# A hybrid decoder trunk on one core: one-pass split products for the index scores, and another order for queries, taps, norm and sparse heads

## The chip, the cores and the metric

The kernel runs on one core of one Trainium2 chip. The metric is the device time of one execution in microseconds (us); the time before is the median of three runs.

## The reference

Two layers over 256 tokens of width 2048, float32. Each layer normalises `x`, multiplies it with one wide input matrix and splits the product into the inputs of three branches and their gates. What the change touches is branch A's token index, the sparse attention behind it, and the place of branch B's norm and branch C's heads around them.

```python
proj = h @ w_in
(qa, ka, va, za, qi, ki, wi, ub, zb, qc, kc, vc, zc, gates) = split(proj)
qa, ka, qi, ki = rope(qa), rope(ka), rope(qi), rope(ki)        # 8, 2, 16 and 1 heads of 128
# A: blocks of 128 queries, each sees the keys up to the block's end
rel   = einsum('bthd,bsd->bhts', qi, ki)                       # 16 index heads, one index key
score = einsum('bhts,bth->bts', relu(rel), wi)
score = where(causal, score, -1e30)
idx   = top_k(score, 64)                                       # each query keeps 64 keys
y_a   = softmax attention of qa over the kept ka, va           # 8 heads, 2 key heads
# B: GLU, causal depthwise conv of 31 taps, LayerNorm, swish
# C: stick-breaking attention, 8 heads
x = x + (g0*(y_a*silu(za)) @ w_a + g1*(y_b*silu(zb)) @ w_b + g2*(y_c*silu(zc)) @ w_c) @ w_out
```

A query among the first 64 has at most 64 causal keys, so it keeps all of them, whatever their scores.

## The kernel before, in words

**Products.** Nearly all matmuls are split products: each operand is written as a high and a low part in a one-pass float32 type (F32R), and a product is high x high + low x high + high x low, three one-pass matmuls that accumulate in PSUM. Weights stream in units of up to 512 KB: a DMA on SP's queue fills a raw buffer (six of them), ScalarE (ACT) casts it to the high part (`high`, L264), VectorE (DVE) subtracts to get the low part (`low`, L269), and TensorE (PE) multiplies (`mult`, L280). High and low parts have three buffers each. `chunk_W`, `chunk_N` give 512 or fewer columns token by token, `chunk_T` gives heads transposed (`rope` rotates these). Small products, those of the index among them (L820), are plain float32 matmuls on unsplit operands.

**Order.** The program order is written out by hand, and a scheduler then orders each engine's instructions by priority. Casts and subtractions run at high priority. Work off the projections goes into three lists. `turns` and `stages` hold generators: after each unit `background` lets one of them go a step (turns first, then the first two stages), bound behind that unit's last matmul; `yield n` asks for n more units. `waiting` holds the 31 taps of the convolution for each half of the channels (`taps`: four ACT scalings L442 and one DVE add L445 each); after a unit's subtraction `drain` issues one of them, unless `hold` is set. `settle`, `finish` and `flush` issue what is left of each list. `turn_in` transposes a chunk with DMAs on SP's queue (L178) between a step before and one after.

**A layer's sequence, as far as the change goes.** Gate and value chunks of branch B and queries, keys, values of branch C (taps begin to drain); four stick generators (two heads each) are started; `hold` is set; index key (2 units), values of A with the index weights (8 units), keys of A (4 units), queries of A (two `chunk_W` of 16 units in all, each turned in and rotated by `spin`, L796 to L798); `finish`; the 16 index query heads as eight `chunk_T` of four units, for the 192 tokens from 64 on, each rotated at once by `rope`; `hold` is lifted; two index generators are started, one for each block of queries; two gate chunks (`early`, 16 units); `finish`; four attention generators (`attend`); two more gate chunks; `flush` of the taps; the conv norm generator; the gates `ZC` and `ZB` (32 units). The index generators take four heads at a step:

```python
for q in range(4):
    nc.tensor.matmul(ps[:, q * n:(q + 1) * n], at(qiT, hd)[:, t * P:(t + 1) * P],
                     kiT[:, 0, :n], start=True, stop=True)      # n = 128 or 256 keys
```

and add each head's relu, times its weight, to the scores; then eight rounds of eight maxima pick the 64 keys. SBUF comes from pools: twelve slots `s8`, eight `t4` temporaries, three `ev`.

Of the kernel before, what the change touches and what calls it, by code (L numbers as in the profile page):

```python
# [15 lines left out]
P = 128  # L16
S = 256
# [37 lines left out]
def trunk(ctx: ExitStack, tc: tile.TileContext, x, xt, w_in, w_a, w_b, w_c, w_out,  # L55
# [33 lines left out]
    sin2 = heads(cst[:, C_SIN:C_SIN + S], 2)  # L89

    uid = [0]

# [73 lines left out]
    def turn_in(src, dst, then=None, slots=True, turn=TURN, early=False):  # L166
        own, cols = words(slots)
        rows = own.rearrange("p (t w d) -> p t w d", t=NT, w=2)
        s16 = src.bitcast(U16).rearrange("p t (d w) -> p t d w", w=2)
        with tc.high_priority():  # L170
            for i in range(2):
                nc.scalar.copy(rows[:, :, i, :], s16[:, :, :, i])

        def steps():
            yield turn[0]
            with tc.high_priority() if turn in MERGED else nullcontext():
                for t in range(NT):
                    nc.sync.dma_start(cols.rearrange("p (g t) -> p g t", g=8)[:, :, t * P:(t + 1) * P],  # L178
                                      own[:, t * 1024:(t + 1) * 1024], transpose=True)
            yield turn[1]  # L180
            halves_ = cols.rearrange("p (w f t) -> p w f t", w=2, f=4)
            into = own.bitcast(F32).rearrange("p (f t) -> p f t", f=4) if dst is None else dst
            d16 = into.bitcast(U16).rearrange("p f (t w) -> p f t w", w=2)
            bound = turn == LATE or turn in MERGED
            with tc.issue_after(lows[0].ins) if bound else nullcontext(), tc.high_priority() if bound else nullcontext():
                nc.vector.tensor_copy(d16[:, :, :, 1], halves_[:, 1])
            with tc.issue_after(highs[0].ins) if bound else nullcontext(), tc.high_priority() if bound else nullcontext():
                (nc.vector.tensor_copy if early else nc.scalar.copy)(d16[:, :, :, 0], halves_[:, 0])
            if dst is None:
                then(into, cols.bitcast(F32).rearrange("p (f t) -> p f t", f=4))  # L190
            elif then is not None:
                then()

        turns.append([steps(), count[0] + 0])
        advance(turns[-1])
# [4 lines left out]
    def finish():  # L200
        while stages:
            advance(stages[0])
# [189 lines left out]
    def split(h, l, src):  # L392
        nc.scalar.copy(h, src)
        nc.vector.tensor_sub(l, src, h.bitcast(F32))
# [1 line left out]
    def pair(n):  # L396
        return tuple(tp.tile([P, n], F32R, tag=t, bufs=2, name=nm(t)) for t in ("ph", "pl"))

    def rope(acc, dst):
        a, a3 = summed(acc)  # L400
        nh, nt = a3.shape[1:]
        sw = ev()[:, :nh * nt]
        with tc.high_priority():
            nc.scalar.copy(sw[0:64, :], a[64:128, :])
# [4 lines left out]
            nc.vector.tensor_add(dst, dst, s3)  # L409

    def sigmoid_of(a):
        sg = ev()
        with tc.high_priority():
            nc.scalar.activation(sg, a, AF.Sigmoid)
        return sg.rearrange("p (h t) -> p h t", h=2)

    def gate(c0, o, b, w, hx, park=None, slots=True, turn=TURN):
        def gated(k, z, v):
# [71 lines left out]
    for layer in range(DEPTH):  # L490
# [288 lines left out]
        va_ = t4(F32R).rearrange("p (i t d) -> p i t d", i=2, t=NT)  # L779
        va = [va_[:, i] for i in range(2)]  # L780
        wi = small(NT * NIH, 2).rearrange("p (t h) -> p t h", t=NT)
        a = chunk_N(w, [(O_VA, 256), (O_WI, NIH)], hx, KD)
        for t in range(NT):
            with tc.high_priority():
                split(va[0][:, t, :], va[1][:, t, :], a[t][:, :256])
                nc.scalar.mul(wi[:, t, :], a[t][:, 256:256 + NIH], WI_SCALE)
        rope(chunk_T(w, O_KA, 256, hx, KD), kaT)

        qaT = slot()
        def spin(q4):  # L790
            for h in range(0, 4, 2):
# [19 lines left out]
        def index(t, qiT=qiT, kiT=kiT, wi=wi, bias=bias):  # L811
            n = (t + 1) * P
            cb = cst[:, C_CB + S - n:C_CB + S]
            sc = tp.tile([P, S], F32, tag="sc", bufs=2, name=nm("sc"))
            bs = tp.tile([P, S], F32, tag="bias", bufs=2, name=nm("bias"))
            for g in range(NIH // 4):
                ps = mm_tile()
                for q in range(4):
                    hd = g * 4 + q
                    nc.tensor.matmul(ps[:, q * n:(q + 1) * n], at(qiT, hd)[:, t * P:(t + 1) * P],  # L820
                                     kiT[:, 0, :n], start=True, stop=True)
                rl = t4()
                nc.scalar.activation(rl[:, :4 * n], ps[:, :4 * n], AF.Relu)
                for q in range(4):
                    hd = g * 4 + q
                    nc.vector.scalar_tensor_tensor(sc[:, :n], rl[:, q * n:(q + 1) * n], wi[:, t, hd:hd + 1],
                                                   cb if hd == 0 else sc[:, :n], op0=ALU.mult, op1=ALU.add)
                yield 2
            for _ in range(TOPK // 8):
                m8 = small(8)  # L830
                nc.vector.max(m8, sc[:, :n])
                nc.vector.match_replace(sc[:, :n], m8, sc[:, :n], TAKEN)
            nc.vector.tensor_scalar(bs[:, :n], sc[:, :n], -2e38, NEG, op0=ALU.is_gt, op1=ALU.mult)
            nc.vector.tensor_tensor(bs[:, :n], bs[:, :n], cb, op=ALU.min)
            bias[t] = bs

        for t in range(NT):
            start(index(t))

        def early(b, j):  # L840
            a = chunk_N(w, [(O_G + b * D + j * 512, 512)], hx, KD)
# [57 lines left out]
        for t in range(NT):  # L899
            for c in range(2):  # L900
                start(attend(t, c))


        for j in range(2, 4):
            early(1, j)
        flush()
        def conv_norm(cv=cv, pr=pr):
            work = t4()
# [22 lines left out]
            for i in range(2):  # L931
# [7 lines left out]
                    nc.vector.tensor_scalar(cs[:, c, :], cs[:, c, :], lw, lb, op0=ALU.mult, op1=ALU.add)  # L939
                nc.vector.tensor_mul(cs, cs, sg.rearrange("p (c t) -> p c t", c=4))  # L940
        start(conv_norm())
        gate(O_ZC, qcT, [], w, hx, parked[2])
        gb = []
        gate(O_ZB, cv, gb, w, hx, slots=False, turn=LATE)
# [308 lines left out]
```

## Time and profile before

| what | value |
|---|---|
| median of 3 runs | 2019.54 us (2019.14 to 2019.95) |
| profiled execution: span from first to last instruction | 2016.9 us |
| PE busy | 2005.8 us (99%) |
| PE weight load busy | 1699.3 us (84%) |
| DVE busy | 1577.9 us (78%) |
| ACT busy | 1388.3 us (69%) |
| POOL busy | 104.8 us (5%) |
| mean granted TensorE clock | 0.999 |

The span runs from the first to the last instruction of the profiled execution; for that execution no other time is given, and the median of the runs is 2.6 us above it. Engines run beside each other, so the shares do not add up. A busy PE is not a PE at its best pace, since matmuls overlap: their pace is read from start to start. A chain row has a start, a duration and what ran; a window row has the stretch, its length, then for each engine busy us and the number of instructions, the clock, the DMA share and GB/s. A group row ends with busy us and the mean ns of one, and the idle time before it.

### The profile page before, as it was taken

How to read it: one execution, taken by the hardware profiler on the slowest of the kernel's cores; microseconds unless marked ns; L12 is line 12 of the kernel's file. 1: busy time of each engine (PE TensorE's matmuls, PEld its weight loads, DVE VectorE, ACT ScalarE, POOL GpSimd, SP SyncE). 2: the span in 40 equal slices, each digit the busy share in tenths (PEclk: the TensorE clock that was granted, in tenths of full speed). 3: DMA queues.
4: the chain of work that ended last, by engine and by line, in shares of the span. 5: the costliest groups of instructions: out<-in, count | busy, mean ns of one | idle time of the engine just before them, and what ended most of it. 6: DMA issues, size and time to landing. Idle time of an engine off the chain costs nothing.

```text
span 2016.9 us, 26722 instructions
## 1 busy us (share of the span) xinstructions
PE 2005.8 (99%) x9550; PEld 1699.3 (84%) x9550; DVE 1577.9 (78%) x1750; ACT 1388.3 (69%) x1952; POOL 104.8 (5%) x160
## 2 busy tenths in 40 slices
PE   9999999999999999999999999999999999999998
PEld 7888889988888888888888888899888888888887
DVE  8688767897798888866676887678967988788665
ACT  7899666687776555556658986676877765555653
POOL 0000000000001200110000000000000012002100
PEclk9999999999999999999999999999999999999999
DMA  8787666656988877889867775676678789768983
GB/s 285 215 227 213 179 178 204 214 178 195 253 237 261 272 245 236 262 267 263 267 198 216 217 211 175 177 205 209 188 206 255 227 261 302 219 230 273 283 268 126
DMA packets 340278, 458.66 MB, mean 227 GB/s; under 512 B 109104, under 2 KB 159024, under 8 KB 340016
## 3 DMA queue, kind: packets, MB, share of 16 engines
q1 hardware_dynamic: 327040, 420.88, 69.7%
q0 software_dynamic: 11648, 33.56, 5.1%
q10 hardware_dynamic: 1456, 2.51, 0.4%
q8 instruction: 75, 1.23, 0.2%
q14 instruction: 59, 0.48, 0.1%
HBM read 413.37 MB, written 20.97 MB: 215 GB/s over the span
## 4 chain that ended last, share of the span: by engine, by line
PE 98%; DMA 1%; DVE 0%; ACT 0%; issue 0%; ACTq 0%; SPq 0%; DVEq 0%
PE acc L280 87%; PE mm L280 8%; PE mm L820 1%; PE mm L857 1%; PE mm L895 0%; PE mm L764 0%; PE mm L728 0%; DMA s<-s 0%; DMA raw<-in_w_in_dram 0%; DVE wl L269 0%; PE mm L750 0%; PE mm L731 0%; PE mm L766 0%; PE mm L755 0%; PE mm L752 0%
## 5 line engine op out<-in xcount | busy, mean ns | idle before, releaser
L280 PE MATMUL acc<-wh,s 128*128 128x512 f32 (+2 forms) x4736 | 1157.0, 386 | 1.2 <-ACT wh L264 1.1
L269 DVE TENSOR_TENSOR wl<-raw,wh 128x1024 fp32r<-128x1024 f32 (+2 forms) x714 | 857.2, 1207 | 294.8 <-ACT wh L264 277.0
L280 PEld LDWEIGHTS acc<-wh,s 128*128 128x128 f32 x4736 | 875.6, 188 | 177.4 <-ACT wh L264 1.5
L264 ACT CAST wh<-raw 128x1024 fp32r<-128x1024 f32 (+2 forms) x713 | 738.8, 1039 | 387.3 <-PE acc L280 304.5
L280 PE MATMUL acc<-wl,s 128*128 128x512 f32 (+2 forms) x2368 | 622.6, 385 | 0.0
L280 PEld LDWEIGHTS acc<-wl,s 128*128 128x128 f32 x2368 | 439.5, 188 | 89.1 <-DVE wl L269 0.2
L442 ACT ACTIVATE t<-s,cst 128x255 f32<-128x255 f32 (+14 forms) x480 | 199.9, 487 | 0.0
L445 DVE TENSOR_TENSOR s<-s,t 128x1020 f32<-128x1020 f32 (+14 forms) x120 | 138.4, 1153 | 0.0
L280 PE MATMUL acc<-s,wh 128*128 128x384 f32 (+1 forms) x608 | 125.8, 348 | 0.0
L280 PE MATMUL mm<-wh,s 128*128 128x512 f32 x448 | 119.7, 389 | 0.0
L280 PEld LDWEIGHTS acc<-s,wh 128*128 128x128 f32 x608 | 104.2, 189 | 3.2
L280 PEld LDWEIGHTS mm<-wh,s 128*128 128x128 f32 x448 | 84.1, 188 | 17.4
L231 POOL COPY sm<-sm 128x3 f32<-128x3 f32 x64 | 52.6, 821 | 544.6 <-ACT sm L230 544.6
L280 PEld LDWEIGHTS acc<-s,wl 128*128 128x128 f32 x608 | 79.0, 191 | 1.9 <-DVE wl L269 0.9
L280 PE MATMUL acc<-s,wl 128*128 128x192 f32 (+1 forms) x608 | 79.5, 273 | 0.6 <-DVE wl L269 0.6
L264 ACT CAST wh<-s 128x1024 fp32r<-128x1024 f32 x32 | 33.6, 1049 | 66.1 <-DVE s L1046 58.6
L280 PE MATMUL mm<-wl,s 128*128 128x512 f32 x224 | 69.1, 390 | 0.0
L264 ACT CAST wh<-t 128x1024 fp32r<-128x1024 f32 x32 | 33.6, 1050 | 40.5 <-DVE t L1046 28.0
L269 DVE TENSOR_TENSOR wl<-s,wh 128x1024 fp32r<-128x1024 f32 x32 | 39.2, 1225 | 24.0 <-ACT wh L264 23.7
L280 PEld LDWEIGHTS mm<-wl,s 128*128 128x128 f32 x224 | 41.9, 188 | 9.0 <-DVE wl L269 0.4
L269 DVE TENSOR_TENSOR wl<-t,wh 128x1024 fp32r<-128x1024 f32 x32 | 39.1, 1222 | 9.9 <-ACT wh L264 7.1
L1046 DVE TENSOR_TENSOR t<-raw,raw 128x1024 f32<-128x1024 f32 x32 | 39.0, 1219 | 0.0
(220 smaller groups left out, 1260.6 us busy)
## 6 DMA issues: line engine op xcount, KB each, us to landing
raw<-in_w_in_dram SPq DMA_DIRECT2D x570, 512.0 KB, 4.4
raw<-in_w_out_dram SPq DMA_DIRECT2D x64, 512.0 KB, 5.1
raw<-in_w_b_dram SPq DMA_DIRECT2D x32, 512.0 KB, 5.1
raw<-in_w_c_dram SPq DMA_DIRECT2D x32, 512.0 KB, 5.2
raw<-in_w_a_dram SPq DMA_DIRECT2D x32, 512.0 KB, 5.3
parked<-s POOLq DMA_DIRECT2D x16, 512.0 KB, 4.7
t<-gates POOLq DMA_DIRECT2D x16, 512.0 KB, 7.0
s<-parked POOLq DMA_DIRECT2D x32, 256.0 KB, 5.7
```

What stands on the lines that cost most here:

```text
L231: seen = nc.gpsimd.tensor_copy(copy[:, :3], mark)
L264: highs[0] = nc.scalar.copy(u[1], u[0])
L269: sub = nc.vector.tensor_sub(u[2], u[0], u[1].bitcast(F32))
L280: newest[0] = nc.tensor.matmul(o, lhsT, rhs, start=start, stop=stop, skip_group_check=True)
L442: nc.scalar.activation(o[:, i, :S - d], yT[:, c, :S - d], AF.Copy, scale=wq)
L445: nc.vector.tensor_add(to, to, o[:, :, :S - d])
L820: nc.tensor.matmul(ps[:, q * n:(q + 1) * n], at(qiT, hd)[:, t * P:(t + 1) * P], kiT[:, 0, :n], start=True, stop=True)
L857: nc.tensor.matmul(ps[:, q * n:(q + 1) * n], qaT[:, c * 4 + q, ts_], kaT[:, c, :n], start=True, stop=True)
L1046: nc.vector.tensor_tensor(o, a_, b_, op=op)
```

## The change

It does four things.

1. The index scores become split products in the one-pass type. Index key and index queries are split into high and low parts; each product is three matmuls. The block of the first 128 queries computes only queries 64 to 127 and puts two heads side by side into one stationary tile (`index_near`); its scores come out on two halves of the partitions and are added. The other block keeps its shape (`index_far`).
2. The rotation of the index queries moves out of `rope` into a generator `rotate`, four heads at a time, whose steps run in `turns`, one after each unit; it ends with the split.
3. The two query chunks of the sparse attention go ahead of the index key, values and keys; `hold` is set only behind all of them, so that taps are drained beside the stick generators.
4. The conv norm generator starts ahead of the attention generators, and the taps are flushed before them.

```diff
-        hold[0] = True
-        kk_ = t4()
-        kaT = kk_[:, :2 * S].rearrange("p (c t) -> p c t", c=2)
-        kiT = kk_[:, 2 * S:3 * S].rearrange("p (c t) -> p c t", c=1)
-        rope(chunk_T(w, O_KI, P, hx, KD), kiT)
...
         for h in range(0, NH, 4):
             turn_in(chunk_W(w, O_QA + h * P, hx), qaT[:, h:h + 4, :], partial(spin, qaT[:, h:h + 4, :]))
+        kaT = t4()[:, :2 * S].rearrange("p (c t) -> p c t", c=2)
+        ki = tp.tile([P, 2 * S], F32R, tag="ki", bufs=1, name=nm("ki")).rearrange("p (i c t) -> p i c t", i=2, c=1)
+        rope(chunk_T(w, O_KI, P, hx, KD), None, partial(split, ki[:, 0], ki[:, 1]))
...
+        wp_ = small(NIH // 2 + 1, 2)[:, :NIH // 2]
+        wf = wi[:, 0, :].rearrange("p (g q) -> p g q", q=2)
+        nc.scalar.copy(wp_[0:64], wf[64:128, :, 0])
+        nc.scalar.copy(wp_[64:128], wf[64:128, :, 1])
+        rope(chunk_T(w, O_KA, 256, hx, KD), kaT)
+
+        hold[0] = True
         finish()
-        qiT = big()
-        for b in qiT:
-            nc.gpsimd.memset(b[:, :, :TOPK], 0.0)
+        qa2 = slot(F32R).rearrange("p a b -> p (a b)").rearrange("p (i h t) -> p i h t", i=2, h=NIH)
+        qb2 = [slot(F32R).rearrange("p a b -> p (a b)").rearrange("p (h t) -> p h t", h=NIH) for _ in range(2)]
+
+        nq = S - TOPK
+
+        def rotate(h, v4):
+            w4 = t4()[:, :4 * nq].rearrange("p (h t) -> p h t", h=4)
+            yield 1
+            nc.scalar.copy(w4[0:64], v4[64:128])
+            nc.scalar.copy(w4[64:128], v4[0:64])
+            nc.vector.tensor_mul(v4, v4, cos4[:, :, TOPK:])
+            yield 1
+            nc.vector.tensor_mul(w4, w4, sin4[:, :, TOPK:])
+            nc.vector.tensor_add(v4, v4, w4)
+            yield 1
+            hs = slice(h, h + 4)
+            nc.scalar.copy(qa2[:, 0, hs, :], v4[:, :, :TOPK])
+            nc.scalar.copy(qb2[0][:, hs, :], v4[:, :, TOPK:])
+            yield 1
+            nc.vector.tensor_sub(qa2[:, 1, hs, :], v4[:, :, :TOPK], qa2[:, 0, hs, :].bitcast(F32))
+            nc.vector.tensor_sub(qb2[1][:, hs, :], v4[:, :, TOPK:], qb2[0][:, hs, :].bitcast(F32))
+
         for h in range(0, NIH, 2):
-            rope(chunk_T(w, O_QI + h * P, 256, hx, KD, TOPK), qiT[h // KC][:, h % KC:h % KC + 2, TOPK:])
+            if h % 4 == 0:
+                v4 = t4()[:, :4 * nq].rearrange("p (h t) -> p h t", h=4)
+            total(chunk_T(w, O_QI + h * P, 256, hx, KD, TOPK), v4[:, h % 4:h % 4 + 2, :])
+            if h % 4:
+                turns.append([rotate(h - 2, v4), count[0]])
+                advance(turns[-1])
+        settle()
         hold[0] = False
...
+        three = ((0, 0), (0, 1), (1, 0))
+
+        def index_near(qa2=qa2, ki=ki, wp_=wp_, bias=bias):
...
+            for g in range(2):
+                ps = mm_tile()
+                for q in range(4):
+                    h = g * 8 + q * 2
+                    for n, (i, j) in enumerate(three):
+                        nc.tensor.matmul(ps[:, q * P:(q + 1) * P], qa2[:, i, h:h + 2, :], ki[:, j, 0, :P],
+                                         start=n == 0, stop=n == 2)
+                rl = t4()
+                nc.scalar.activation(rl[:, :4 * P], ps[:, :4 * P], AF.Relu)
+                for q in range(4):
+                    nc.vector.scalar_tensor_tensor(sc[:, :P], rl[:, q * P:(q + 1) * P],
+                                                   wp_[:, g * 4 + q:g * 4 + q + 1], sc[:, :P],
+                                                   op0=ALU.mult, op1=ALU.add)
+                yield 2
...
+        def index_far(qb2=qb2, ki=ki, wi=wi, bias=bias):
...
             for g in range(NIH // 4):
                 ps = mm_tile()
                 for q in range(4):
-                    hd = g * 4 + q
-                    nc.tensor.matmul(ps[:, q * n:(q + 1) * n], at(qiT, hd)[:, t * P:(t + 1) * P],
-                                     kiT[:, 0, :n], start=True, stop=True)
+                    for n, (i, j) in enumerate(three):
+                        nc.tensor.matmul(ps[:, q * S:(q + 1) * S], qb2[i][:, g * 4 + q, :], ki[:, j, 0, :],
+                                         start=n == 0, stop=n == 2)
...
+        start(index_near())
+        start(index_far())
...
-        for t in range(NT):
-            for c in range(2):
-                start(attend(t, c))
-
-
-        for j in range(2, 4):
-            early(1, j)
         flush()
...
         start(conv_norm())
+        for t in range(NT):
+            for c in range(2):
+                start(attend(t, c))
+
+
+        for j in range(2, 4):
+            early(1, j)
         gate(O_ZC, qcT, [], w, hx, parked[2])
```

More of the change, by code (lines that the diff above doesn't have):

```diff
@@ L89, in trunk @@
     sin2 = heads(cst[:, C_SIN:C_SIN + S], 2)
+    cos4 = heads(cst[:, C_COS:C_COS + S], 4)
+    sin4 = heads(cst[:, C_SIN:C_SIN + S], 4)
     uid = [0]
@@ L397, in pair, with rope @@
         return tuple(tp.tile([P, n], F32R, tag=t, bufs=2, name=nm(t)) for t in ("ph", "pl"))
-    def rope(acc, dst):
+    def rope(acc, dst, halves=None):
         a, a3 = summed(acc)
         nh, nt = a3.shape[1:]
+        dst = a3 if dst is None else dst
         sw = ev()[:, :nh * nt]
@@ L409, in rope @@
             nc.vector.tensor_add(dst, dst, s3)
[L411 to L415, printed above, removed]
+            if halves is not None:
+                halves(dst)
     def gate(c0, o, b, w, hx, park=None, slots=True, turn=TURN):
@@ L772, in trunk @@
             start(stick(h0))
-        hold[0] = True
-        kk_ = t4()
-        kaT = kk_[:, :2 * S].rearrange("p (c t) -> p c t", c=2)
-        kiT = kk_[:, 2 * S:3 * S].rearrange("p (c t) -> p c t", c=1)
-        rope(chunk_T(w, O_KI, P, hx, KD), kiT)
[L779 to L782, printed above, removed]
-        for t in range(NT):
[L784 to L787, printed above, removed]
         qaT = slot()
@@ new lines, in trunk @@
+        rope(chunk_T(w, O_KI, P, hx, KD), None, partial(split, ki[:, 0], ki[:, 1]))
+        va_ = t4(F32R).rearrange("p (i t d) -> p i t d", i=2, t=NT)
+        va = [va_[:, i] for i in range(2)]
+        wi = small(NT * NIH, 2).rearrange("p (t h) -> p t h", t=NT)
+        a = chunk_N(w, [(O_VA, 256), (O_WI, NIH)], hx, KD)
+        for t in range(NT):
+            with tc.high_priority():
+                split(va[0][:, t, :], va[1][:, t, :], a[t][:, :256])
+                nc.scalar.mul(wi[:, t, :], a[t][:, 256:256 + NIH], WI_SCALE)
@@ L808, in trunk, with chosen @@
+        for h in range(0, NIH, 2):
+            if h % 4 == 0:
[5 more added lines that the diff above has]
+        settle()
         hold[0] = False
         bias = {}
-        def index(t, qiT=qiT, kiT=kiT, wi=wi, bias=bias):
-            n = (t + 1) * P
-            cb = cst[:, C_CB + S - n:C_CB + S]
+        def chosen(sc, bs, cb):
+            for _ in range(TOPK // 8):
+                m8 = small(8)[-sc.shape[0]:]
+                nc.vector.max(m8, sc)
+                nc.vector.match_replace(sc, m8, sc, TAKEN)
+            nc.vector.tensor_scalar(bs, sc, -2e38, NEG, op0=ALU.is_gt, op1=ALU.mult)
+            nc.vector.tensor_tensor(bs, bs, cb, op=ALU.min)
@@ new lines, in trunk @@
+        three = ((0, 0), (0, 1), (1, 0))
+        def index_near(qa2=qa2, ki=ki, wp_=wp_, bias=bias):
+            cb = cst[:, C_CB + P:C_CB + S]
+            sc = tp.tile([P, S], F32, tag="sc", bufs=2, name=nm("sc"))
+            bs = tp.tile([P, S], F32, tag="bias", bufs=2, name=nm("bias"))
+            nc.vector.tensor_copy(sc[:, :P], cb)
+            nc.vector.memset(sc[:TOPK, :P], 0.0)
+            for g in range(2):
[12 more added lines that the diff above has]
+                yield 2
+            near, even = sc[TOPK:, :P], sc[TOPK:, P:]
+            nc.scalar.copy(even, sc[:TOPK, :P])
+            nc.vector.tensor_add(near, near, even)
+            nc.vector.tensor_copy(bs[:TOPK, :P], cb[:TOPK])
+            chosen(near, bs[TOPK:, :P], cb[TOPK:])
+            bias[0] = bs
@@ L814, in index @@
+        def index_far(qb2=qb2, ki=ki, wi=wi, bias=bias):
+            cb = cst[:, C_CB:C_CB + S]
             sc = tp.tile([P, S], F32, tag="sc", bufs=2, name=nm("sc"))
@@ L818, in index @@
                 for q in range(4):
-                    hd = g * 4 + q
-                    nc.tensor.matmul(ps[:, q * n:(q + 1) * n], at(qiT, hd)[:, t * P:(t + 1) * P],
-                                     kiT[:, 0, :n], start=True, stop=True)
+                    for n, (i, j) in enumerate(three):
+                        nc.tensor.matmul(ps[:, q * S:(q + 1) * S], qb2[i][:, g * 4 + q, :], ki[:, j, 0, :],
+                                         start=n == 0, stop=n == 2)
                 rl = t4()
-                nc.scalar.activation(rl[:, :4 * n], ps[:, :4 * n], AF.Relu)
+                nc.scalar.activation(rl, ps, AF.Relu)
                 for q in range(4):
                     hd = g * 4 + q
-                    nc.vector.scalar_tensor_tensor(sc[:, :n], rl[:, q * n:(q + 1) * n], wi[:, t, hd:hd + 1],
-                                                   cb if hd == 0 else sc[:, :n], op0=ALU.mult, op1=ALU.add)
+                    nc.vector.scalar_tensor_tensor(sc, rl[:, q * S:(q + 1) * S], wi[:, 1, hd:hd + 1],
+                                                   cb if hd == 0 else sc, op0=ALU.mult, op1=ALU.add)
                 yield 2
[L829 to L838, printed above, removed]
+            chosen(sc, bs, cb)
+            bias[1] = bs
+        start(index_near())
+        start(index_far())
         def early(b, j):
@@ L897, in attend @@
             nc.scalar.copy(qaT[:, c * 4:c * 4 + 4, ts_], po[:, :512].rearrange("p (h t) -> p h t", h=4))
-        for t in range(NT):
-            for c in range(2):
-                start(attend(t, c))
-        for j in range(2, 4):
-            early(1, j)
         flush()
@@ L941, in trunk @@
         start(conv_norm())
+        for t in range(NT):
+            for c in range(2):
+                start(attend(t, c))
+        for j in range(2, 4):
+            early(1, j)
         gate(O_ZC, qcT, [], w, hx, parked[2])
```

## The prediction

> **What bounds the kernel now.** I read the page first: span, busy shares, shares of the chain that ended last.
>
> ```profile
> span 2016.9 us, 26722 instructions
> PE 2005.8 (99%) x9550; PEld 1699.3 (84%) x9550; DVE 1577.9 (78%) x1750; ACT 1388.3 (69%) x1952; POOL 104.8 (5%) x160
> PE 98%; DMA 1%; DVE 0%; ACT 0%; issue 0%; ACTq 0%; SPq 0%; DVEq 0%
> ```
>
> PE carries 98% of the chain. Then the waits, PE's own (all there are) and two of ACT's:
>
> ```profile
> PE acc L280 <- ACT wh L264: 1.1, 1, 1.1
> PE mm L625 <- DVE eps L76: 1.1, 1, 1.1
> PE acc L280 <- DVE wl L269: 0.6, 1, 0.6
> ...
> ACT wh L264 <- PE acc L280: 314.1, 254, 3.4
> ACT wh L264 <- DMA raw<-in_w_in_dram: 8.1, 6, 1.7
> ```
>
> PE waits 2.8 us in all, 2.2 of it at the start. The casts of ACT wait for PE to give a weight buffer back (314.1 us), hardly for a load (8.1 us). So a matmul taken out of PE's stream is worth its pace, and work on ACT, DVE, POOL or SP is worth nothing until it makes PE wait. The execution is the profiled one, 2016.9 us of span; the median of the runs is 2019.54, so 2.6 us lie around the span. I apply differences to the median.
>
> **The sum on PE.** The chain shows the index products (L820) between the units of the gate projection, the groups their number, and the timeline the pace of one-pass products.
>
> ```profile
> 389.76 0.89 PE mm L820 x8
> 390.65 2.73 PE acc L280 x12
> 393.38 1.73 PE mm L820 x8
> ...
> 303.17 0.24 PE mm L752 x2
> ```
> ```profile
> L820 PE MATMUL mm<-t,s 128*128 128x256 f32 x64 | 15.1, 378 | 0.0
> L820 PE MATMUL mm<-t,s 128*128 128x128 f32 x64 | 8.4, 274 | 0.0
> ```
> ```profile
> 384.53 1.59 PE L280 MATMUL acc<-s,wh 128*128 128x384 f32 x8
> ...
> 385.95 1.03 PE L280 MATMUL acc<-s,wl 128*128 128x192 f32 x8
> ...
> 386.82 2.03 PE L280 MATMUL acc<-wh,s 128*128 128x512 f32 x8
> 387.15 0.47 ACT L305 COPY ev<-acc 128x384 f32<-128x384 f32 x1
> ...
> 389.60 1.05 PE L820 MATMUL mm<-t,s 128*128 128x128 f32 x8
> ...
> 392.50 0.56 DVE L409 TENSOR_TENSOR s<-s,ev 128x384 f32<-128x384 f32 x1
> ```
>
> A group of four heads is four products, and a plain float32 product leaves two records, so eight records make a group: 0.89 us for 128 keys, 1.73 us for 256. Four groups of each per layer: 4 x (0.89 + 1.73) = 10.48 us. The one-pass type is known at 256 columns: two L752 in 0.24 us, 0.12 each. At 192 columns eight take 386.82 - 385.95 = 0.87 us, 0.109 each; at 384 eight take 385.95 - 384.53 = 1.42 us, 0.178 each. From 384 to 256 the pace falls 0.058, from 256 to 192 by only 0.011: below 256 something other than the columns limits, and 0.109 is nearly the floor.
>
> After, the far block (queries 128 to 255) is 16 heads x 3 products of 256 columns: 48 x 0.12 = 5.76 us. The near block computes only queries 64 to 127 (the first 64 keep all their causal keys), two heads side by side in one stationary tile: 8 pairs x 3 products of 128 columns. No row shows a one-pass product of 128 columns. From below, the line through 384 and 256 gives 0.12 - 0.058 = 0.062; from above, one plain product of 128 columns, 0.89/4 = 0.222. I take 0.109, since 192 columns are nearest and flat: 24 x 0.109 = 2.62 us. Per layer 8.38 against 10.48, 2.10 saved; in two layers **4.2 us**. With the ends: 24 x 2 x 0.047 = 2.3 us more, or 24 x 2 x 0.113 = 5.4 us less.
>
> All other PE work (projections, sticks, attention, conv mean) keeps its count and only changes order.
>
> **The moves, and what hides them.** Stage by stage in layer 1 (columns: span, then PE, PEld, DVE, ACT, POOL busy): the later half of the value and gate units with taps, then the sticks stage, the index-query projection, the two gate chunks with the index, the rest; then the same for the taps' ACT instructions alone.
>
> ```profile
> 1080.00:1200.00 120.00, 120.00 (x531) 99.34 (x530) 97.52 (x88) 119.63 (x225) 0.00 (x0) 1.00 0.77 216
> ...
> 1230.50:1313.20 82.70, 82.70 (x450) 72.11 (x448) 56.72 (x71) 57.77 (x74) 0.53 (x1) 1.00 0.64 188
> 1313.20:1387.00 73.80, 73.80 (x516) 73.76 (x516) 60.59 (x74) 51.12 (x67) 0.00 (x0) 1.00 0.74 223
> 1387.00:1431.40 44.40, 44.40 (x215) 37.62 (x214) 40.91 (x78) 36.05 (x65) 0.73 (x1) 1.00 0.54 166
> 1431.40:1560.00 128.60, 128.60 (x577) 106.79 (x576) 99.76 (x127) 98.81 (x154) 4.37 (x7) 1.00 0.78 222
> ```
> ```profile
> 1230.50:1313.20 82.70, 1.85 (x4) 1.00 0.64 188
> ...
> 1387.00:1431.40 44.40, 15.56 (x38) 1.00 0.54 166
> 1431.40:1560.00 128.60, 11.15 (x28) 1.00 0.78 222
> ```
>
> *Taps run on.* The 15.56 + 11.15 = 26.7 us of taps that today run after the index queries move beside the sticks: ACT there goes from 57.8 to 84.5 us in 82.7 us, full. Each tap also brings a DVE add:
>
> ```profile
> L445 DVE TENSOR_TENSOR s<-s,t 128x1020 f32<-128x1020 f32 (+14 forms) x120 | 138.4, 1153 | 0.0
> ```
>
> 66 tap instructions are 16.5 taps, 16.5 x 1.15 = 19 us, DVE from 56.7 to 75.7. I cost this at nothing because the stage before it ran with ACT at 119.63 of 120 us and PE never waited: casts go ahead, taps yield. What spills (2 us, some more with the chains of the sticks) falls into the query stage, where ACT has 22.7 us free. From a cover gone the bounds are zero and the spill twice, 4 us. In return the index stage loses taps: DVE 40.9 of 44.4 falls by some 9, ACT by 15.6.
>
> *Rotation in steps.* Per four heads today: ACT 2 x (0.47 + 0.51 + 0.51) = 3.0, DVE 2 x (0.55 + 3 x 0.56) = 4.5. After, with 768-wide operations and a split into high and low parts:
>
> ```profile
> L756 DVE TENSOR_TENSOR t<-t,mm 128x768 f32<-128x768 f32 x2 | 1.9, 948 | 0.0
> L759 DVE TENSOR_TENSOR t<-t,cst 128x256 f32<-128x256 f32 x4 | 1.5, 422 | 1.8 <-ACT t L757 1.8
> ...
> L404 ACT COPY ev<-ev 64x384 f32<-64x384 f32 x8 | 4.1, 512 | 6.3 <-DVE ev L306 6.2
> L757 ACT ACTIVATE t<-t 128x768 f32<-128x768 f32 x2 | 1.7, 847 | 4.3 <-DVE t L756 4.3
> L768 ACT COPY s<-mm 128x512 f32<-128x512 f32 x2 | 1.1, 606 | 0.0
> ```
>
> ACT 2 x 0.47 + 2 x 0.85 + about 0.4 + 0.61 = 3.65; DVE 2 x 0.55 + 3 x 0.95 + 0.42 + about 0.65 = 5.0. Four times per layer: ACT +2.6 of 22.7 us free, DVE +2.2 of 13.2 free. Nothing, while that room lasts. What is late next is the last rotation, whose steps all come at once when the projection ends. Today the last one ends 392.50 + 0.56 - 387.15 = 5.9 us after its first copy, while the first index product already runs at 389.60: products wait for their own heads only. After, the chain to the near block's second half is 0.47 + 0.55 + 1.7 + 3 x 0.95 + 0.4 + 0.42 = 6.4 us bare. Today 0.47 + 0.55 + 1.02 + 2 x 0.56 = 3.2 us bare became 5.9 with casts between; the same 2.7 us on top gives 9.1, the same proportion 11.8. Its cover: three units of 2.73 and groups of 24 x 0.109/2 = 1.3 and 12 x 0.12 = 1.4, 10.9 us. So zero to 0.9 us a layer; I take 0.2, as the middle of the two still fits.
>
> *Sparse queries ahead of the keys.* 16 units go before 14 with the same loads. Four transposing DMAs per layer pass the key, value and weight loads on SP's queue.
>
> ```profile
> SPq L178 <- ACT wh L264: 33.4, 21, 3.0
> ```
>
> Such a DMA holds SP at most 3.0 us; a unit takes 2.7 and six raw buffers are ahead, so nothing. A gain is possible: the 0.6 us wait of layer 0 comes from the second query rotation on DVE in front of the projection's subtractions.
>
> ```profile
> 331.24 0.68 DVE L797 TENSOR_TENSOR ev<-ev,cst 128x512 f32<-128x512 f32 x1
> 331.84 1.21 DVE L269 TENSOR_TENSOR wl<-raw,wh 128x1024 fp32r<-128x1024 f32 x1
> ...
> 333.11 1.14 PE L280 MATMUL acc<-s,wl 128*128 128x192 f32 x8 [0.60 <-DVE wl L269]
> ```
>
> That rotation comes 14 units earlier after the change. Taps may take its place; I count half, -0.3.
>
> *Norm ahead of sparse heads.* The conv norm takes the place of one attention group; its DVE and ACT work moves into the room that the taps left, and the attention's six transposing DMAs come later but still within the 48 units of gates around them. Nothing, between 0 and 1 us. The two memsets on POOL per layer go: nothing. Splitting the index key and packing 16 weights adds a few operations of 256 columns or less (0.42 us in the row above) in the sticks stage: covered as the taps are.
>
> Sum: -4.2 - 0.3 + 2 x 0.2 = -4.1; 2019.5 - 4.1 gives **2015.4 us**, own range 2014.4 to 2016.4: the 0.6 us wait kept or gone, the last rotation at 0 or 0.9.
>
> **The rivals.** *A, narrow products faster* (faster): nothing but columns limits, 0.062 us each, 2.3 us more: 2013.1. The flat step from 256 to 192 speaks against it. The Trainium skill, "TensorE: Matmul & The Clock Gate", section "Back-to-back issue gap", gives about 81 ns for a matmul of 128 columns in a stream; by it the estimate would be 1.3 us lower, 2014.1. The same page's section "LDWEIGHTS (loading the stationary operand)" has columns over 1.2, 107 ns for 128, which the trace's 109 for 192 columns bears out. Chance 0.06.
>
> *B, narrow products not one-pass* (same): 0.222 us each, 5.4 us lost: 2020.8. Against it: 192 columns run at 0.109. Chance 0.05.
>
> *C, the saving is given back* (same): the last rotation holds the near block's second half, or the full ACT a stick's step, for 0.5 to 2 us a layer: 2016.4 to 2019.4. For it: cover 10.9 against 9 to 12, and ACT without slack. Chance 0.29.
>
> *D, casts fall behind taps* (slower). With sticks and taps together ACT is beyond its stage by 2 us and loses the lead of three weight buffers; each moved tap then delays a cast by one of its four ACT instructions, 26.7/66 = 0.40 us: 33 taps in two layers, 13 us, 2028.8. It ends above 2023.6 (slower by 0.2%) from (4.1 + 4.0)/33 = 0.25 us per tap. Against it the 120 us at full ACT without a wait; for it the sticks, whose DVE steps wait for ACT in the same queue as the subtractions. Chance 0.10. The Trainium skill, "TensorE: Matmul & The Clock Gate", section "Architectural detail: the array is 16× 32×32, not 1× 128×128", calls the queues of ScalarE and VectorE strict first-in first-out; by that rule a late step holds what stands behind it, the condition of this rival.
>
> **How the numbers follow.** Forecast 0.50, A 0.06, B 0.05, C 0.29, D 0.10. About 0.2%, 4.0 us, is what a measurement of this kernel can tell from no change: faster is below 2015.5. The forecast lies only 0.1 us under that line; I give 0.08 of its chance to same, not half, because layer 1 shows the order without any wait. Faster 0.42 + 0.06 = 0.48, same 0.08 + 0.05 + 0.29 = 0.42, slower 0.10. The range 2013.8 to 2019.5 leaves out A's lower part, B and D, 0.2.
>
> **What would show it.** 24 and 48 one-pass index products per layer, paced 0.109 and 0.12, pieces of 1.3 and 1.4 us in the chain; a 128-column pace of 0.06 or 0.22 would show A or B. No taps after the index-query projection and ACT at 97% or more of the sticks stage; PE's waits still below 1 us there (D: a list of waits for casts or subtractions). Before the near block's second half no gap, else C. The wait of 0.6 us in layer 0 gone or moved. The prediction fails if PE's waits grow by more than 4 us.

## The result: 1% slower

The changed kernel takes 2040.08 us (median of 4 runs, 2039.56 to 2041.4) against 2019.52; the ratio is 1.0104 [1.0089, 1.0118], 20.6 us slower, outside the range. In the changed kernel the line numbers are shifted: the projections' matmuls are L282, the subtraction L271, the cast L266, the near and far index products L859 and L883, the stick heads' last products L763 and L765, the attention's value products L953, the taps L441 and L444. First its page, then all waits of PE (total us, times, longest).

```profile
span 2037.8 us, 26759 instructions
...
PE 2010.5 (99%) x9566; PEld 1701.6 (84%) x9566; DVE 1584.0 (78%) x1736; ACT 1397.2 (69%) x1960; POOL 101.7 (5%) x156
...
PE 92%; ACT 3%; DVE 2%; issue 1%; DMA 1%; SPq 0%; ACTq 0%; DVEq 0%
```
```profile
PE mm L763 <- DVE t L758: 9.2, 2, 4.6
PE mm L953 <- DVE pl L396: 4.2, 2, 2.2
PE mm L749 <- ACT ph L395: 1.2, 2, 0.6
PE mm L727 <- ACT s L767: 1.1, 2, 0.6
PE mm L624 <- DVE eps L76: 1.1, 1, 1.1
PE mm L749 <- DVE pl L396: 1.0, 2, 0.5
PE mm L529 <- DVE t L649: 0.7, 1, 0.7
PE acc L282 <- ACT wh L266: 0.4, 1, 0.4
```

PE's busy share reads 99% before and after, and DVE's and ACT's shares hardly move; only the chain (98% PE, now 92%) and the waits tell of the loss. PE's waits add up to 18.9 us, 16.1 more than the 2.8 before; by the prediction's own sign, more than 4 us, it failed. The index products did what was forecast; the chain of layer 0:

```profile
399.46 1.29 PE mm L859 x12
400.75 2.82 PE acc L282 x12
403.57 1.42 PE mm L883 x12
404.99 2.76 PE acc L282 x12
407.74 1.29 PE mm L859 x12
```

1.29/12 = 0.108 us and 1.42/12 = 0.118 us a product. Per layer 2 x 1.29 + 4 x 1.42 = 8.26 us against 10.48, so 4.4 us are saved in two layers, and no gap stands before the near block's second half. The span grew by 20.9 us: -4.4 from the products, +16.1 of waits, and 9.2 us that remain; slower products behind the waits are most of those (below). The largest wait, layer 0, from the timelines of PE and DVE:

```profile
318.83 0.36 PE L282 MATMUL acc<-s,wl 128*128 128x192 f32 x2
...
319.12 0.68 DVE L412 TENSOR_TENSOR t<-t,ev 128x512 f32<-128x512 f32 x1
319.73 0.69 DVE L782 TENSOR_TENSOR s<-s,ev 128x512 f32<-128x512 f32 x1
320.33 1.81 DVE L755 TENSOR_TENSOR t<-t,mm 128x768 f32<-128x768 f32 x2
322.06 1.22 DVE L271 TENSOR_TENSOR wl<-raw,wh 128x1024 fp32r<-128x1024 f32 x1
323.19 1.43 DVE L758 TENSOR_TENSOR t<-t,cst 128x256 f32<-128x256 f32 x4
...
323.76 1.19 PE L763 MATMUL mm<-t,s 128*128 128x256 f32 x2 [4.57 <-DVE t L758]
```

PE stops in the middle of a unit, since the last stick heads' products come next in its order. What they wait for (L755 on DVE, an exponent on ACT, L758 on DVE) stands on DVE behind the key rotation (L412) and the sparse query rotation (L782). Then the slow stretch: a row of the chain after and the same row of before (L764 there), and the windows of the sticks stage, the 20 us behind it, the rest of the index-query projection and the index stage:

```profile
325.38 0.85 PE mm L763 x2
```
```profile
310.12 0.43 PE mm L764 x2
```
```profile
228.80:312.80 84.00, 82.36 (x445) 71.37 (x444) 68.91 (x82) 80.37 (x138) 0.00 (x0) 1.00 0.68 173
312.80:333.00 20.20, 15.63 (x86) 14.77 (x85) 16.95 (x26) 11.86 (x17) 0.00 (x0) 0.83 0.34 98
333.00:396.00 63.00, 63.00 (x442) 63.00 (x441) 46.87 (x50) 37.74 (x47) 0.00 (x0) 1.00 0.75 226
396.00:440.00 44.00, 44.00 (x233) 37.77 (x232) 39.34 (x89) 24.48 (x29) 0.85 (x1) 1.00 0.57 168
```

The same two records take 0.85 us instead of 0.43: half the pace, with a granted clock of 0.83 over the window. In layer 1 the clock is 0.83 too, from 1320 to 1340 us. Together these two windows lose at most 0.17 x 20.2 + 0.17 x 20 = 6.8 of the 9.2 us; some 2 us stay open. In the last two windows PE never waits. The Trainium skill, "TensorE: Matmul & The Clock Gate", section "What's actually happening", lets the clock fall to half after an idle window of about 3.4 us; the wait of 4.57 us with the half pace behind it agrees.

### The profile page after: what moved, and what is told of

The parts are those of the page before. It is cut to its first block, busy times and chain, and to the rows that moved or that the text cites. A ratio compares the mean times of both kernels' runs of the same rounds, so it can differ in the third digit from the quotient of the medians.

```text
span 2037.8 us, 26759 instructions
## 1 busy us (share of the span) xinstructions
PE 2010.5 (99%) x9566; PEld 1701.6 (84%) x9566; DVE 1584.0 (78%) x1736; ACT 1397.2 (69%) x1960; POOL 101.7 (5%) x156
## 4 chain that ended last, share of the span: by engine, by line
PE 92%; ACT 3%; DVE 2%; issue 1%; DMA 1%; SPq 0%; ACTq 0%; DVEq 0%
PE acc L282 81%; PE mm L282 7%; ACT wh L266 1%; DVE wl L271 1%; PE mm L883 1%; PE mm L915 1%; DMA t<-t 0%; PE mm L763 0%; PE mm L953 0%; DMA raw<-in_w_in_dram 0%; PE mm L727 0%; ACT t L441 0%; PE mm L859 0%; DMA s<-s 0%; PE mm L765 0%
## 5 line engine op out<-in xcount | busy, mean ns | idle before, releaser
L282 PE MATMUL acc<-wh,s 128*128 128x512 f32 (+2 forms) x4736 | 1155.4, 386 | 0.5 <-ACT wh L266 0.4
L271 DVE TENSOR_TENSOR wl<-raw,wh 128x1024 fp32r<-128x1024 f32 (+1 forms) x714 | 859.0, 1208 | 314.6 <-ACT wh L266 304.5
L282 PEld LDWEIGHTS acc<-wh,s 128*128 128x128 f32 x4736 | 875.8, 188 | 177.5 <-ACT wh L266 1.5
L266 ACT CAST wh<-raw 128x1024 fp32r<-128x1024 f32 (+1 forms) x713 | 739.4, 1039 | 410.8 <-PE acc L282 337.0
L282 PE MATMUL acc<-wl,s 128*128 128x512 f32 (+2 forms) x2368 | 623.3, 385 | 0.0
L282 PEld LDWEIGHTS acc<-wl,s 128*128 128x128 f32 x2368 | 439.6, 188 | 88.9
L441 ACT ACTIVATE t<-s,cst 128x255 f32<-128x255 f32 (+14 forms) x480 | 198.9, 487 | 0.0
L444 DVE TENSOR_TENSOR s<-s,t 128x1020 f32<-128x1020 f32 (+14 forms) x120 | 138.6, 1155 | 1.5 <-ACT t L441 1.1
L282 PE MATMUL acc<-s,wh 128*128 128x384 f32 (+1 forms) x608 | 125.5, 347 | 0.0
L282 PE MATMUL mm<-wh,s 128*128 128x512 f32 x448 | 119.7, 389 | 0.0
L282 PEld LDWEIGHTS acc<-s,wh 128*128 128x128 f32 x608 | 104.2, 189 | 3.1
L282 PEld LDWEIGHTS mm<-wh,s 128*128 128x128 f32 x448 | 84.1, 188 | 17.4
L282 PEld LDWEIGHTS acc<-s,wl 128*128 128x128 f32 x608 | 80.0, 192 | 0.9
L282 PE MATMUL acc<-s,wl 128*128 128x192 f32 (+1 forms) x608 | 80.4, 274 | 0.0
L266 ACT CAST wh<-s 128x1024 fp32r<-128x1024 f32 x32 | 33.6, 1050 | 66.0 <-DVE s L1104 59.3
L282 PE MATMUL mm<-wl,s 128*128 128x512 f32 x224 | 69.1, 390 | 0.0
L904 POOL DMA_DIRECT2D gates<-t x8 | 6.0, 744 | 1123.1 <-ACT t L903 1123.1
L266 ACT CAST wh<-t 128x1024 fp32r<-128x1024 f32 x32 | 33.6, 1050 | 41.2 <-DVE t L1104 27.4
L271 DVE TENSOR_TENSOR wl<-s,wh 128x1024 fp32r<-128x1024 f32 x32 | 39.2, 1225 | 24.0 <-ACT wh L266 23.8
L282 PEld LDWEIGHTS mm<-wl,s 128*128 128x128 f32 x224 | 41.9, 188 | 9.0 <-DVE wl L271 0.4
L271 DVE TENSOR_TENSOR wl<-t,wh 128x1024 fp32r<-128x1024 f32 x32 | 39.1, 1222 | 9.9 <-ACT wh L266 7.1
```

The source lines that it names most:

```text
L266: highs[0] = nc.scalar.copy(u[1], u[0])
L271: sub = nc.vector.tensor_sub(u[2], u[0], u[1].bitcast(F32))
L282: newest[0] = nc.tensor.matmul(o, lhsT, rhs, start=start, stop=stop, skip_group_check=True)
L441: nc.scalar.activation(o[:, i, :S - d], yT[:, c, :S - d], AF.Copy, scale=wq)
L444: nc.vector.tensor_add(to, to, o[:, :, :S - d])
L904: nc.gpsimd.dma_start(gates[b][:, :, j * 512:(j + 1) * 512].rearrange("t p d -> p t d"), sg_)
```

## The experiments

Theories: **T**, the taps fill ACT and DVE beside the stick heads; **O**, the queries ahead of the keys put other work onto the last stick heads; **N**, the norm ahead delays the attention. Each kernel was timed beside the kernel before. "us" is the median.

| run | us | ratio [95%] |
|---|---|---|
| e1 taps held | 2052.27 | 1.0162 [1.0147, 1.0177] |
| e2 queries back | 2035.57 | 1.0079 [1.0064, 1.0094] |
| e3 norm back | 2032.35 | 1.0062 [1.0045, 1.0078] |
| e4 index only | 2028.07 | 1.0038 [1.0025, 1.0052] |
| e5 order, no taps | 2023.39 | 1.0020 [1.0011, 1.0030] |
| e6 index, no taps | 2019.37 | 1.0001 [0.9991, 1.0010] |
| e7 no finish | 2022.75 | 1.0018 [1.0008, 1.0027] |
| e8 queries and norm back | 2029.40 | 1.0051 [1.0036, 1.0066] |
| e9 rotation bound | 2033.42 | 1.0072 [1.0057, 1.0087] |
| e10 taps later | 2034.60 | 1.0080 [1.0065, 1.0095] |
| e11 taps later, rotation bound | 2033.27 | 1.0069 [1.0052, 1.0086] |
| e12 no finish, rotation bound | 2026.68 | 1.0035 [1.0022, 1.0048] |
| e13 e6, rotation bound | 2016.29 | 0.9984 [0.9975, 0.9994] |
| e14 e5, rotation bound | 2029.92 | 1.0051 [1.0036, 1.0066] |
| e15 taps at queries | 2020.03 | 1.0003 [0.9994, 1.0013] |
| e16 taps shared | 2025.83 | 1.0030 [1.0017, 1.0042] |
| e17 e15, no finish | 2015.47 | 0.9982 [0.9973, 0.9991] |
| e18 e17, taps from the keys | 2015.83 | 0.9983 [0.9974, 0.9992] |

**One part undone each (e1 to e4).**

```diff
 # e1: hold ahead of the sparse queries
+        hold[0] = True
         for h in range(0, NH, 4):
             turn_in(chunk_W(w, O_QA + h * P, hx), ...)
 # e2: those two lines moved behind rope(chunk_T(w, O_KA, ...), kaT)
 # e3: start(attend) and early(1, 2..3) moved ahead of flush() and conv_norm again
 # e4: e2 and e3, and hold[0] = True ahead of the index key: the old order
```

> The changed kernel, only the hold is set ahead of the sparse query chunks again, so that no tap is drained beside the stick heads; the order of the projections stays changed. Theory T (the taps fill ACT and make the last stick heads late): the wait of 4.6 us per layer at the last stick products and the half clock behind it go, the index products keep their 4.3 us, what is left is the attention's wait: about 2021 us, PE's waits below 8 us. Theory O (the queries ahead of the keys put their rotations and the short value units onto the last stick heads): the wait stays at 3 us or more per layer, at least 2032 us.

> The changed kernel with the sparse query chunks behind the keys again; the taps still run beside the stick heads. Theory O: the wait at the last stick products goes, about 2021 us. Theory T: ACT is as full as in the changed kernel, the wait stays at 3 us or more per layer, at least 2032 us.

> The changed kernel with the attention heads started ahead of the two gate chunks and the conv norm behind them, as before. Theory N (the norm ahead of the sparse heads makes their transposed probabilities late): the wait of 2.2 us per layer at the attention's value products goes and with it some us at a lower clock, 2034 to 2036 us. If the wait has another cause (taps, or the index): it stays, about 2040 us.

> The split index products and the rotation in steps alone; projections, hold, attention and norm stand in the order of before. Theory (the product arithmetic was right and only the reordering costs): 2015 us, 48 products per layer... at 0.118 and 24 at 0.11 us, PE's waits below 3.5 us. Rival (the rotation in steps itself makes work late): 2018 us or more, with waits in the index stage.

e3 bears out N, at a higher price than I gave: 7.7 us. PE's waits account for 4.1 of it (18.9 less 14.8 us); the clock does not explain the rest, since behind this wait it stays at 1.00 in both layers (519.7 to 539.7 and 1526 to 1546 us). In the changed kernel's timeline PE waits for an attention product whose input comes off a DMA, and ahead of that DMA a table load and sigmoids of a gate chunk (L903) stand on ACT:

```profile
512.23 1.28 ACT L903 ACT_TABLE_LOAD   x1
...
516.08 1.24 SPq L936 DMA_TRANSPOSE t<-t  x1
...
521.29 0.45 DVE L944 COPY t<-t 128x512 uint16<-128x512 uint16 x1 [2.51 <-DMA t<-t]
521.64 0.68 DVE L396 TENSOR_TENSOR pl<-t,ph 128x512 fp32r<-128x512 f32 x1
...
522.38 0.50 PE L953 MATMUL mm<-pl,t 128*128 128x512 f32 x1 [2.21 <-DVE pl L396]
```

That the norm's place brings the wait is shown by e3; how is not: e3 has the same table load (at 511.46 us) and sigmoids, and PE does not wait for the attention there.

e1 fits neither theory: without taps beside them the waits at the stick products fell from 9.2 us to 4.0, 2.0 per layer, where T had them gone and O had 3 or more; but the held taps came later, PE waited for the conv norm's sums (8.5 us), subtractions (5.1) and the gates' sigmoids (4.7), and the kernel became slower still. e2 settled nothing cleanly either: its time is T's, but the stick wait fell to 0.9 us, and a new one of 3.1 us per layer came up between index key and values. Its row in the list of PE's waits, then its DVE timeline:

```profile
PE acc L282 <- DVE ev L308: 6.1, 2, 3.1
```
```profile
257.41 1.23 DVE L271 TENSOR_TENSOR wl<-raw,wh 128x1024 fp32r<-128x1024 f32 x1
258.56 2.32 DVE L444 TENSOR_TENSOR s<-s,t 128x952 f32<-128x952 f32 x2
260.80 1.22 DVE L271 TENSOR_TENSOR wl<-raw,wh 128x1024 fp32r<-128x1024 f32 x1
261.93 0.68 DVE L308 TENSOR_TENSOR ev<-acc,ev 128x512 f32<-128x512 f32 x1
```

Two taps' adds and a subtraction stand ahead of the addition that empties a PSUM buffer. e4 is the surprise: split index and rotation in steps alone, in the order of before, cost 8.5 us, as the rival had it. Its wait in the index stage, from the timelines of DVE and PE:

```profile
424.83 1.22 DVE L271 TENSOR_TENSOR wl<-raw,wh 128x1024 fp32r<-128x1024 f32 x1
426.08 0.29 DVE L841 MAX8 sm<-sc 64x8 f32<-64x128 f32 x1
426.41 1.14 DVE L444 TENSOR_TENSOR s<-s,t 128x944 f32<-128x944 f32 x1
...
428.00 0.48 DVE L889 SCALAR_TENSOR_TENSOR sc<-t,sm,sc 128x256 f32<-128x256 f32 x1
...
431.38 1.23 DVE L271 TENSOR_TENSOR wl<-raw,wh 128x1024 fp32r<-128x1024 f32 x1
...
432.66 1.20 PE L282 MATMUL acc<-wl,s 128*128 128x512 f32 x4 [2.57 <-DVE wl L271]
```

From one subtraction to the next 6.55 us pass, filled with a tap (L444), maxima (L841) and score sums of the far block (L889), while a unit takes 2.73 us. Split and rotation were not tried apart.

**Taps left out, or no forced last step (e5 to e8).**

```diff
 # e5 (on e3): hold ahead of the sparse queries; e6 (on e4): hold where it is; in both
+        waiting.clear()
 # e7 (on e3): ahead of the index queries
-        finish()
 # e8: e2 and e3 together
```

> The kernel of e3 (norm back behind the attention, queries still ahead of the keys), with the hold set ahead of the queries and the some 18 taps per layer that are then still waiting left out altogether: no tap runs beside the stick heads or later. Theory O (the order alone makes the last stick heads late): the waits at the stick products stay at 2.5 us or more per layer, 2022 us or more. Theory T (the taps make them late): they go, 2016 to 2018 us.

> The kernel of e4 (split index and rotation in steps, the old order) with the some 18 taps per layer that are held behind the index queries left out. Theory (its waits of 2.7 us per layer in the index stage come from taps and the index's operations together on DVE): they go, 2018 us with the waits that are left at the start of the query projection. Rival (the index's new operations alone make the subtractions late): the waits stay, 2024 us or more.

> The kernel of e3 without the finish ahead of the index queries: the last steps of the stick heads come off the units of the index-query projection instead of at once. Theory (the last stick products stand too close behind the work that feeds them): the wait of 4.6 us per layer at them and the lower clock behind it go, 2017 to 2021 us. Rival (ACT and DVE are late as a whole): the wait goes over to casts or subtractions, 2027 us or more.

> Queries behind the keys and norm behind the attention, as before; split index, rotation in steps and taps beside the stick heads as in the changed kernel. If the norm's share adds up with e2's: 2035.6 - 7.7 = 2028 us, with 3 us per layer of waits between index key and values. If the parts act on each other: 2031 us or more, or 2025 us or less.

Here one edit at a time has a price (e5, e6, e13 and e14 do 18 taps per layer less work). Taps beside the sticks: e3 less e5, 9.0 us. Queries ahead: 4.0 us without taps (e5 less e6), 3.0 with them (e3 less e8). Norm ahead, in the other order: e2 less e8, 6.2 us. Taps behind the index queries: e4 less e6, 8.7 us. So T and O both hold, T with the larger share: e5 has the time of O, but its stick waits, 2.0 us per layer, lie between the two. e6, at 2019.4 rather than 2018, keeps a wait of 1.5 us per layer at the start of the index-query projection. e7, between its theory and the rival, took 9.6 us off by a single deleted line; 1.6 us per layer stayed at the stick products. e8 comes within 1.4 us of the plain sum of 2028.

**The rotation bound to the units; taps later (e9 to e12).** In the changed kernel only PE's matmuls of a step are bound to its unit, not DVE's and ACT's part (some copies of the attention are the exception). These kernels bind the query rotation:

```diff
 # spin: a generator in turns, two steps per pair of heads
+                    with tc.issue_after(highs[0].ins):
                         nc.scalar.copy(s3[0:64], a3[64:128])
                         nc.scalar.copy(s3[64:128], a3[0:64])
+                    with tc.issue_after(lows[0].ins):
                         nc.vector.tensor_mul(a3, a3, cos2)
 # e9 on e3, e12 on e7.  e10 on e4, e11 with the rotation bound too:
-        hold[0] = False          # behind the index queries
         for j in range(0, 2):
             early(1, j)
         finish()
+        hold[0] = False
```

> The kernel of e3 with the rotation of the sparse queries cut in four steps per chunk, each bound behind the newest cast and subtraction of its engine. Theory (the two query rotations stand on DVE ahead of the last stick heads' subtraction and exponent): the wait at the last stick products falls from 4.6 us per layer to below 2, 2021 to 2026 us. Rival (the taps or the stick heads' own chain is late, not the rotations): the wait stays above 3.5 us, 2030 us or more.

> The kernel of e4 (split index, old order) with the hold of the taps kept until the index is finished, so that the last 18 taps run beside the attention. Theory (what cost e4 its 8.7 us against e6 is taps and index operations on DVE in one stage): 2019 to 2020 us, only the waits of the query projection's start left. Rival (the taps cost wherever they fall in this kernel): 2024 us or more.

> The kernel of e10 with the rotation of the sparse queries in bound steps as in e9. Theory (the wait of 1.7 us per layer at the start of the query projection comes from these rotations standing between subtractions): it goes, and the product arithmetic shows whole: 2015 to 2016.5 us, faster than the kernel before. Rival: the wait only moves, 2018 us or more.

> The kernel of e7 (queries ahead, taps beside the sticks, norm back, no finish ahead of the query projection) with the rotation of the sparse queries in bound steps. If e7's remaining wait of 1.6 us per layer at the last stick products comes from these rotations: 2018 to 2020 us. If it comes from taps and the short value units: 2022 us or more.

All four missed the theory's time and came out at the rival's. In e9 the stick wait halved, but a wait of 3.3 us per layer appeared where ACT empties the values' PSUM buffer, and the time did not fall:

```profile
PE acc L282 <- ACT sm L805: 6.6, 2, 3.3
PE mm L763 <- DVE t L758: 4.6, 4, 2.1
```

(L805 scales the index weights out of that buffer.) In e12 the same wait took the place of e7's and made the time 3.9 us worse. e10 shows that later is no better for the taps: beside the attention they cost 15.2 us (e10 less e6), as waits at its products and behind a chunk's evacuation:

```profile
PE mm L953 <- ACT ph L395: 5.7, 2, 2.9
PE acc L282 <- ACT s L174: 4.2, 2, 2.1
```

In e11 the projection's wait for subtractions fell from 3.0 to 0.5 us, as meant; the attention's waits stayed.

**What is left without taps, and a place for them (e13 to e18).**

```diff
 # e13: e6, rotation bound.  e14: e5, rotation bound
 # e15: e4 with rotation bound, and
+        hold[0] = False
         for h in range(0, NH, 4):
             turn_in(chunk_W(w, O_QA + h * P, hx), ...)
+        hold[0] = True
 # e16: hold[0] = h > 0 inside that loop.  e17: e15, and
-        finish()                 # ahead of the index queries
 # e18: e17 with hold[0] = False ahead of the keys of A
```

> The kernel of e6 (split index, old order, the some 18 held taps per layer left out) with the rotation of the sparse queries in bound steps. Theory (the split index itself saves its 4.3 us wherever DVE has room): its last waits, 1.7 us per layer, go, 2015 to 2016 us. Rival (the split index brings waits of its own): 2018 us or more.

> The kernel of e5 (queries ahead of the keys, norm back, those taps left out) with the rotation of the sparse queries in bound steps. If the order's own 8 us come from the query rotations standing on DVE ahead of the last stick heads: 2016 to 2018 us, no wait above 0.5 us at the stick products. If they come from the shorter time between the stick heads' steps: waits of 2 us or more per layer stay, 2020 us or more.

> Split index in the old order, rotation of the sparse queries in bound steps, and the held taps drained beside the sparse query chunks (16 units) alone, not beside keys and values. Theory (taps cost where DVE and ACT are full; here the wait of e8 between index key and values goes, with its waits at the query projection): 2016 to 2020 us. Rival (any taps beside the stick heads make them late): 2024 us or more.

> As e15, but taps are drained beside the first of the two query chunks (8 units) and the rest behind the index queries. Theory (each stage has room for some eight taps): 2015 to 2018 us. Rival: e4's wait of 2.7 us per layer in the index stage stays, 2022 us or more.

> The kernel of e15 without the finish ahead of the index queries, so that the last stick heads' steps come off that projection's units. Theory (e15's 1.8 and 0.4 us per layer at the last stick products are the forced last step, as in e7): they go, 2015.5 to 2017 us, faster than the kernel before by 0.1 to 0.2%. Rival (DVE and ACT are late there whatever the step): 2019 us or more.

> As e17, the taps drained from the keys of A on, 20 units instead of 16, so that none is left for the index stage. If the four taps left there cost nothing, the time is e17's; if the stick stage has no more room, waits at the stick products or casts add 1 us per layer or more.

e13 is 3.0 us faster than the kernel before (2019.29 there): with those taps left out and the rotation bound, most of the 4.4 us shows. e14 felled my form of O, that the query rotation alone is in the way: bound, it made the stick wait worse, 10.6 us in place of 4.0. Its timeline at the first of these waits:

```profile
316.88 0.68 DVE L411 TENSOR_TENSOR ev<-ev,cst 128x512 f32<-128x512 f32 x1
317.48 0.68 DVE L788 TENSOR_TENSOR s<-s,ev 128x512 f32<-128x512 f32 x1
318.08 0.68 DVE L412 TENSOR_TENSOR t<-t,ev 128x512 f32<-128x512 f32 x1
318.68 0.75 DVE L758 TENSOR_TENSOR t<-t,cst 128x256 f32<-128x256 f32 x2
...
319.15 1.22 PE L763 MATMUL mm<-t,s 128*128 128x256 f32 x2 [4.59 <-DVE t L758]
```

The rotation of A's keys (L411, L412, at high priority) stands there beside the queries' (L788): with the queries ahead the keys come last before the stick heads' forced step. But e5 has the same key rotation there (L411 at 317.41 us, L412 at 318.12), so it does not explain the difference. What differs is that in e5 the middle products of both last generators (L749) have run by 312.7 us, while in e14 the last generator's run only at 321.73, behind the wait. The bound rotation stands in `turns`, whose steps go first and take units off which the stick heads would have gone on; that this is the cause was not tried. e15 and e16 tell place from amount: half as many taps beside the sticks (e16) leave a wait in the index stage as in e4 (up to 3.1 us), nearly all of them beside the query chunks (e15) only a wait at the stick products, 3.7 us in all. **e17** takes the forced step away and beats both kernels: 2015.47 against 2019.28 us, 0.9982 [0.9973, 0.9991], with these waits of PE in all:

```profile
PE mm L624 <- DVE eps L76: 1.1, 1, 1.1
PE acc L282 <- ACT wh L266: 0.6, 1, 0.6
PE mm L529 <- DVE t L649: 0.6, 1, 0.6
PE acc L282 <- DVE wl L271: 0.5, 2, 0.2
```

2.8 us, as in the kernel before. e18 is the same within the interval: four more taps beside the sticks find room.

## Why the prediction was wrong

- **Right: the sum on PE.** 0.109 and 0.12 us were forecast, 0.108 and 0.118 measured; 4.2 us forecast, 4.4 measured. Rivals A and B are out: the Trainium skill's 81 ns ("TensorE: Matmul & The Clock Gate", "Back-to-back issue gap") does not hold for these products. e17 takes 2015.47 us, but it is another kernel: that it meets the forecast of 2015.4 bears out this sum, not the forecast for the changed kernel.
- **Right: no gap at the near block's second half; the 0.6 us wait of layer 0 gone; no tap behind the index queries.** ACT reached 80.37 of 84.0 us of the sticks stage, 96% where I said 97 or more.
- **Right, in the changed kernel: "Nothing, while that room lasts" for the rotation and the split.** PE is busy for all of the 63.0 and 44.0 us of the windows of the query projection and the index stage above, so the 0.4 us put down for the last rotation were not needed either. The room is thin: in e4, with the taps back in the index stage, PE waits up to 2.6 us there while DVE is busy for 43.9 of 48.5 us. A mean over such a window does not say that a subtraction comes every 2.7 us.
- **Wrong: "I cost this at nothing because the stage before it ran with ACT at 119.63 of 120 us and PE never waited".** That stage has taps and projections alone, and the casts go ahead of the taps. Beside the sticks the taps cost 9.0 us. The work there is a chain over DVE, ACT and DVE (L755 to L758 above) that ends in a product which PE meets in a fixed order, and each link stands behind what was put ahead of it. A full engine was harmless where the only due work on it went first, and not where such a chain ran on it.
- **Wrong: "16 units go before 14 with the same loads ... so nothing."** I passed the queue of SP in review, but not DVE's: both query rotations and the key rotation fell onto the last stick heads. 3 to 4 us.
- **Wrong: "Nothing, between 0 and 1 us" for the norm.** 7.7 us (6.2 in the other order), 4.1 of it PE's waits; what in the norm's steps makes the attention late stays open.
- **Wrong: the sum's own range.** With the 0.6 us wait gone and the last rotation at nothing its terms give 2019.5 - 4.2 - 0.6 = 2014.7 us, with the wait kept and 0.9 us a layer 2017.1, not 2014.4 to 2016.4.
- **Rivals.** C named the right thing, the saving given back, but at 0.5 to 2 us a layer where it was some 12.6 ((20.9 + 4.4)/2), because I priced a wait at its length and left out the slow clock behind it, and because I put 1 us where several moves add up in one place. D had the sign, not the mechanism: in the changed kernel PE waits 0.4 us for casts and none for subtractions.

How the parts add up along one path: norm 7.7 (to e3), taps 9.0 (to e5), queries 4.0 (to e6), unbound rotations of the sparse queries 3.1 (to e13), together 2040.08 - 2016.29. In another order the shares differ by 1 to 1.6 us (queries 3.0, norm 6.2), which the scatter of the runs could make as well: those of e2 lie 3.1 us apart, those of e8 3.9. That parts act on each other shows in the bound rotation: it saves 3.1 us in the old order (e6 to e13) and costs 6.5 with the queries ahead (e5 to e14). Why each engine's order came out as it did was not tried.

## What to carry to other kernels

Where one engine is full and the others run beside it, a busy share says little on whether moved work is free: list for each moved step what stands next to it in the queue, and when the product behind it is due. Undo the parts one at a time, and both ways: some eighteen taps per layer cost 9.0 us beside the stick heads, 8.7 behind the index queries, 15.2 beside the attention and 3.7 beside the query chunks (e15 less e13); with the forced step gone too, e17 has them and is not slower than e13, which leaves them out. A forced completion ahead of a stage (`finish`) turns a late chain into a wait; letting it run off the next stage's units took 9.6 us off here with one line, and 4.6 in the old order (e15 to e17).

## What the hardware showed that I had not expected

A wait can cost more than its length. Behind waits of 2 to 5 us the granted clock in 20 us windows fell to 0.91 or 0.83, though not each time. In e10 (its two layers' evacuation wait of 2.1 us) and e4 (2.6 us), windows of 20 us from just before the wait:

```profile
1520.00:1540.00 20.00, 17.90 (x73) 14.37 (x72) 11.90 (x14) 18.29 (x31) 0.73 (x1) 0.91 0.85 230
```
```profile
425.00:445.00 20.00, 17.43 (x77) 14.13 (x76) 19.59 (x39) 17.32 (x35) 0.66 (x1) 1.00 0.63 186
```

If the pace was half, as in the rows of the result, a clock of 0.91 over 20 us is by estimate 0.09 x 20 x 2 = 3.6 us of slow products, 1.8 us lost. So a wait of 2.1 us can be followed by it and one of 2.6 us not, nor e10's own wait of 2.8 us at 541 us (clock 1.00 from 537 to 557); the 3.4 us of idleness that the Trainium skill names (page and section as above) were not needed in e10.
